# The first stage of a fixed-order decoder layer: squares summed by the matrix product alone, x scaled early, loads on one queue

## The chip, the core and the metric

The kernel runs on one core of one Trainium2 chip, in one launch. TensorE (PE) does the matrix products, ScalarE (ACT) and VectorE (DVE) the elementwise work; DMA transfers are issued by SyncE (SP) and GpSimd (POOL). The metric is the time of one execution on the device in microseconds (us): the median of three runs before the change is 2008.87 us (2008.06 to 2016.31). One execution was profiled: 2006.7 us, of which the span of the trace takes 2004.6 us.

## The reference

One layer of a hybrid decoder on 1024 prompt tokens (one sequence) and 32 sample tokens (8 sequences of 4), width 1024, all in float32. A conditioning vector per sequence gives scale and shift of every norm:

```python
mod = (jax.nn.silu(c) @ w_ada + b_ada).reshape(B, N_MOD, D_MODEL)
hn = modulate(rmsnorm(x, g_ffn1), mod[:, 0], mod[:, 1])       # h * (1 + scale) + shift
x = x + 0.5 * mod[:, 2][:, None, :] * swiglu(hn, w1_gate, w1_up, w1_down)
hn = modulate(rmsnorm(x, g_mix), mod[:, 3], mod[:, 4])
mo, ... = mixer(hn, ...)                                      # recurrence and short convolution
x = x + mod[:, 5][:, None, :] * mo
hn = modulate(rmsnorm(x, g_ffn2), mod[:, 6], mod[:, 7])
x = x + 0.5 * mod[:, 8][:, None, :] * swiglu(hn, w2_gate, w2_up, w2_down)
y = rmsnorm(x, final_gain)
```

`rmsnorm` divides by the root of the mean square over the 1024 channels; `swiglu` is silu(h·Wg)·(h·Wu), times Wd, with 3072 hidden channels.

## The kernel before

Tokens lie along the free dimension (N = 1056, two halves of 528), channels along the 128 partitions in 8 blocks k. Every float32 operand of a large product is split into a high part (ACT copies it, rounded) and a low part (DVE subtracts), and a product is three matrix products: high·high, high·low, low·high. A weight unit of 128x512 is split in the same way (`split_to`, L218 on ACT and L219 on DVE). The hidden channels of the first feed-forward layer are computed in pairs of column blocks. Pairs 1 to 11 go by Strassen's scheme with seven products each (`strassen`, L441): the forms of the activations are, in order, 11, T1, T2, 22, T3, 21, T4 (11, 22 and 21 are quarters of the activations themselves, T1 to T4 are sums of quarters), those of the weights 11, S1, S2, S4, S3, 12, 22, and the seven go into three accumulators a, c, a, c, a, b, a, named `ga_` for the gate and `up_` for the up product. Pair 0 is done directly, in `first_pair()` (L877); the products of its two column blocks are called `first` and `second` in the trace.

`first_pair()` is the first stage, and what the change touches. In the order of the code:

- x is loaded in three pieces (352, 528 and 176 tokens) on POOL's queue (L919); the conditioning weights (`ada`) and the first weights (`wf`) come on SP's queue.
- `norm` (L889): for each block k ACT squares a piece of x (L528), DVE adds the squares into one accumulator (L532, L537), and PE sums it over the partitions with one-column matmuls, three for the first piece, five and two for the others (`nrm`, L551). `stats` then takes mean, root and reciprocal (L554 to L559), puts it on diagonals (`dg`, L565), spreads it over the partitions with a matmul (`rb`, L572), and ACT copies it out (`rall`, L576).
- the conditioning products (`ada`, L485), their transpose and sum into `modT` (L490 to L500).
- for each block k `modulate`: DVE multiplies x by scale and norm in one instruction (L613), ACT adds the shift and rounds to the high part (L615), DVE makes the low part (L616), ACT adds the shift to x itself (L618). The products of this block follow (L906). Blocks 0 and 1 use the first conditioning part, blocks 2 to 4 the second, 5 to 7 the third.
- the silu of the gate (L924, ACT) and the product with up (L926, DVE); T1 and T2 (`token_forms`, L650 to L656) and T3 (`rest_of_forms`); the products of the second column block; its silu and product; T4.

The order in which each engine meets its instructions is set by a scheduler of the framework from dependences and estimated times, not by the order of the code. On each engine instructions then run in that order.

Of the kernel before, what the change touches and what calls it, by code (L numbers as in the profile page):

```python
# [1 line left out]

# [235 lines left out]
def decoder_step(ctx, tc, xin, par, ada0, ada1, ada2, wada, wf, wga, wdn, wdl, wmi, wgt, wmo,  # L238
# [77 lines left out]

    def prompt(span):

        return min(span[0] + span[1], T) - span[0]
# [204 lines left out]
    def square_add(accs, sp, k, new=tmp, fold=False, join=False):  # L524

        xs = x[:, k, of(sp)]
        sq = new(f"sq{sp[0]}_{k}", sp[1])
# [7 lines left out]
        if fold and k == KD - 1:  # L535
            for other in (accs.pop(), accs.pop()):
                dve.tensor_add(accs[0], accs[0], other)  # L537
# [3 lines left out]
    def stats(accs, spans, first, lag, keep=None):  # L541
# [6 lines left out]
        b = bank(f"nrm{name}")  # L548
        for i, (c, s, _) in enumerate(at):
            for n, acc in enumerate(accs[c]):  # L550
                pe.matmul(b[:, i:i + 1], acc[:, s:s + P], ones[:, 0:1], start=n == 0, stop=n == len(accs[c]) - 1)  # L551
# [26 lines left out]
    def modulate_samples(buf, k0, k1, sp, inplace=False):  # L578

        if inplace and (len(x.cuts(k0, k1)) > 1 or k0 < 4 < k1):  # L580
            for a, e in x.cuts(k0, k1):
                for lo, hi in ((a, min(e, 4)), (max(a, 4), e)):
                    if lo < hi:
                        modulate_samples(buf, lo, hi, sp, True)
# [9 lines left out]
        for a, e in x.cuts(k0, k1):  # L594
# [282 lines left out]
    def first_pair():  # L877
        fp = open_pool("firstp", bufs=10)
        firstp.append(fp)
        rall = fp.tile([P, N], F32, name="rall", bufs=1)  # L880
        early, late = FIRST_SPANS[:-1], FIRST_SPANS[-1:]
# [3 lines left out]
        def square(name, width):  # L885
            return fp.tile([P, CH], F32, tag="sq", name=name, bufs=5)[:, :width]

        def norm(spans):
            accs = []  # L889
            for sp in spans:  # L890
                accs.append([])
                for k in range(KD):
                    square_add(accs[-1], sp, k, square, True)
            for _ in stats(accs, spans, 0, 0, keep=rall):
                pass
# [7 lines left out]
        def product(outs, spans, hl, k, j, first, last):  # L903
            for i, (wh, h) in enumerate(((0, 0), (0, 1), (1, 0))):
                for sp in spans:
# [3 lines left out]
        def products(spans, ks, ahead):  # L909
            for k in ks:  # L910
                for w in range(2):
                    product(outs[w], spans, ws.unit(gu[k // 4][w], ahead), k, k % 4, k == 0, k == KD - 1)
# [5 lines left out]
        def load(lo, n):  # L918
            pool.dma_start(x[:, :, lo:lo + n], xin[:, :, lo:lo + n])  # L919

        def swiglu(j, outs):
            m = [(wide if j == 0 else lambda name: tmp(name, HALF))(f"m{j}_{h}") for h in range(2)]
            for sp in FIRST_SPANS:
                act.activation(piece(m, sp), outs[0][sp], AF.Silu)  # L924
            for sp in FIRST_SPANS:
                dve.tensor_mul(piece(m, sp), piece(m, sp), outs[1][sp])  # L926
            return m

        load(0, 352)
        load(352, 528)  # L930
        load(*late[0])
        ada_stream(fp, KD, range(NFIRST), lambda u: (ada0, ada1, ada2)[u[0]][u[1]])
# [11 lines left out]
        lo, n = late[0][0], prompt(late[0])  # L944
        for u in range(NFIRST):
            k1 = k0 + ADA[u][0][4]
            ks = range(k0, k1)
            if u == 0:
                for last, spans in enumerate((early[:1], early[1:])):
                    for k in ks:  # L950
                        for sp in spans:
                            modulate(0, k, sp[0], sp[1], rall[:, of(sp)])
                        if last and k == k1 - 1:
                            norm(late)
                        products(spans, [k], 1)
                        more_ada(2)
                modulate_samples(0, k0, k1, late[0], True)
                for k in ks:
                    modulate(0, k, lo, n, rall[:, lo:T])
                    products(late, [k], 1)  # L960
                ws.raw_bufs = 2
                ws.dma_ahead()
            else:
                modulate_samples(0, k0, k1, late[0], True)
                for k in ks:
                    for a, e in ((0, HALF), (HALF, T)):
                        modulate(0, k, a, e - a, rall[:, a:e])
                    products(FIRST_SPANS, [k], 3 if k >= 4 else 1)
                    if k == k0 and u + 1 < NFIRST:
                        more_ada(KD)  # L970
# [4 lines left out]
        m0 = swiglu(0, outs)  # L975
        forms = {f: form_tile(f, f"hn{f}") for f in ("T1", "T2", "T3")}
        forms.update({"11": hns[0][0][0], "21": hns[0][1][0], "22": hns[0][1][1]})
        for _ in token_forms(forms, 0, HALF):
            pass
        rest_of_forms(forms, ["T3"])  # L980
        outs = [outputs(f"second{w}_") for w in range(2)]
        for w in range(2):
            ids = ws.take("gu1", (1, w))
            for k in range(KD):
# [472 lines left out]
```

## Time and profile before

| | |
|---|---|
| median of three runs | 2008.87 us (2008.06 to 2016.31) |
| profiled execution | 2006.7 us, its span 2004.6 us |
| PE busy | 1942.3 us, 97% of the span |
| DVE, ACT, POOL busy | 1284.5, 768.7, 128.7 us |
| chain of work that ended last | PE 93%, DVE 4%, DMA 2% |
| mean granted clock of PE over the span | 0.991 of full speed |

PE's granted clock is given in tenths or as a share of full speed; its two levels are 1.2 and 2.4 GHz, so 0.50 is the lower and 1.00 the upper. In the page's 40 slices, 50 us each, PE is below nine tenths only in the first two (three and seven tenths) and the last one; DMA moves most in the first slice (278 GB/s). The first stage ends at about 124 us of the span, where the Strassen products of pair 1 begin.

### The profile page before, as it was taken

How to read it: one execution, taken by the hardware profiler on the slowest of the kernel's cores; microseconds unless marked ns; L12 is line 12 of the kernel's file. 1: busy time of each engine (PE TensorE's matmuls, PEld its weight loads, DVE VectorE, ACT ScalarE, POOL GpSimd, SP SyncE). 2: the span in 40 equal slices, each digit the busy share in tenths (PEclk: the TensorE clock that was granted, in tenths of full speed). 3: DMA queues.
4: the chain of work that ended last, by engine and by line, in shares of the span. 5: the costliest groups of instructions: out<-in, count | busy, mean ns of one | idle time of the engine just before them, and what ended most of it. 6: DMA issues, size and time to landing. Idle time of an engine off the chain costs nothing.

```text
span 2004.6 us, 36544 instructions
## 1 busy us (share of the span) xinstructions
PE 1942.3 (97%) x15188; PEld 1912.5 (95%) x15188; DVE 1284.5 (64%) x2549; ACT 768.7 (38%) x1366; POOL 128.7 (6%) x226
## 2 busy tenths in 40 slices
PE   3799999999999999999999999999999999999997
PEld 2699999999999999999999999999999999999997
DVE  4934555565457875584887768666555645878656
ACT  4523223233343422244443447433333333433324
POOL 0000000110010100000000010001000000100000
PEclk8899999999999999999999999999999999999999
DMA  7145545541254523011111122533323223742402
GB/s 278 50 161 172 188 165 177 184 139 65 75 183 163 194 74 130 22 48 53 48 43 53 43 78 76 179 130 106 114 81 102 92 86 107 245 149 92 140 33 87
DMA packets 88773, 230.68 MB, mean 115 GB/s; under 512 B 7792, under 2 KB 40576, under 8 KB 88608
## 3 DMA queue, kind: packets, MB, share of 16 engines
q1 hardware_dynamic: 62512, 133.07, 19.9%
q0 software_dynamic: 26096, 95.28, 13.2%
q8 instruction: 119, 1.95, 0.4%
q14 instruction: 46, 0.38, 0.1%
HBM read 180.63 MB, written 47.69 MB: 114 GB/s over the span
## 4 chain that ended last, share of the span: by engine, by line
PE 93%; DVE 4%; DMA 2%; ACT 1%; issue 0%; SPq 0%; DVEq 0%; ACTq 0%
PE bk L402 14%; PE up_a L441 13%; PE ga_a L441 13%; PE dn_a L441 9%; PE up_c L441 6%; PE ga_c L441 6%; PE dn_c L441 5%; PE ga_b L441 3%; PE up_b L441 3%; PE v L402 2%; PE b L402 2%; PE c L402 2%; PE x L402 2%; PE n L402 2%; PE dn_b L441 2%; PE ada L485 2%
## 5 line engine op out<-in xcount | busy, mean ns | idle before, releaser
L219 DVE TENSOR_TENSOR hl<-raw,hl 128x512 fp32r<-128x512 f32 x286 | 195.0, 686 | 213.5 <-ACT hl L218 213.1
L218 ACT ACTIVATE hl<-raw 128x512 fp32r<-128x512 f32 x286 | 175.9, 625 | 261.3 <-PE bk L402 105.2
L218 ACT ACTIVATE hl<-S_ga 128x512 fp32r<-128x512 f32 x176 | 111.0, 631 | 272.4 <-DVE S_ga L171 55.0
L441 PE MATMUL dn_a<-f,hl 128*128 128x264 f32 x1536 | 191.8, 284 | 0.0
L402 PE MATMUL bk<-ml,hl 128*128 128x352 f32 (+2 forms) x1248 | 189.5, 312 | 2.1 <-DVE x L672 2.1
L441 PEld LDWEIGHTS dn_a<-f,hl 128*128 128x128 f32 x1536 | 189.2, 188 | 0.0
L402 PEld LDWEIGHTS bk<-ml,hl 128*128 128x128 f32 x1248 | 186.5, 188 | 2.6 <-DVE x L672 2.6
L219 DVE TENSOR_TENSOR hl<-S_ga,hl 128x512 fp32r<-128x512 f32 x176 | 121.2, 689 | 84.2 <-ACT hl L218 83.4
L672 DVE SCALAR_TENSOR_TENSOR x<-bk,modT,x 128x352 f32<-128x352 f32 (+6 forms) x160 | 81.3, 533 | 101.1 <-PE bk L402 100.3
L441 PE MATMUL up_a<-hnT,hl 128*128 128x264 f32 x792 | 102.6, 285 | 0.0
L441 PE MATMUL ga_a<-hnT,hl 128*128 128x264 f32 x792 | 102.5, 285 | 0.0
L441 PE MATMUL up_a<-hmT,hl 128*128 128x264 f32 x792 | 102.3, 285 | 0.0
L441 PE MATMUL ga_a<-hmT,hl 128*128 128x264 f32 x792 | 102.3, 285 | 0.0
L441 PEld LDWEIGHTS up_a<-hnT,hl 128*128 128x128 f32 x792 | 98.7, 188 | 2.5 <-ACT u5st L455 0.4
L441 PEld LDWEIGHTS ga_a<-hnT,hl 128*128 128x128 f32 x792 | 98.6, 188 | 2.5 <-ACT g1st L455 0.4
L441 PEld LDWEIGHTS ga_a<-hmT,hl 128*128 128x128 f32 x792 | 98.9, 188 | 0.4 <-ACT g1st L455 0.4
L441 PEld LDWEIGHTS up_a<-hmT,hl 128*128 128x128 f32 x792 | 98.9, 188 | 0.4 <-ACT u1st L455 0.4
L441 PE MATMUL dn_c<-f,hl 128*128 128x264 f32 x768 | 96.4, 284 | 0.0
L441 PEld LDWEIGHTS dn_c<-f,hl 128*128 128x128 f32 x768 | 94.8, 188 | 0.0
L806 DVE TENSOR_TENSOR f<-f 128x1056 fp32r<-128x1056 f32 x56 | 67.9, 1253 | 26.0 <-ACT f L805 26.0
L218 ACT ACTIVATE hl<-S_dn 128x512 fp32r<-128x512 f32 x64 | 40.0, 629 | 112.1 <-PE dn_a L441 30.4
L528 ACT ACTIVATE sq<-x 128x352 f32<-128x352 f32 (+4 forms) x120 | 50.3, 434 | 71.5 <-DVE x L672 52.1
(447 smaller groups left out, 3740.2 us busy)
## 6 DMA issues: line engine op xcount, KB each, us to landing
raw<-wga SPq DMA_DIRECT2D x88, 512.0 KB, 3.4
f<-mf POOLq DMA_DIRECT2D x28, 1056.0 KB, 5.9
raw<-wada SPq DMA_DIRECT2D x56, 512.0 KB, 5.0
raw<-wdn SPq DMA_DIRECT2D x32, 512.0 KB, 3.4
mf<-mt POOLq DMA_DIRECT2D x48, 264.0 KB, 3.3
raw<-wmi SPq DMA_DIRECT2D x20, 512.0 KB, 3.3
ml<-ml POOLq DMA_DIRECT2D x16, 528.0 KB, 5.2
raw<-wdl SPq DMA_DIRECT2D x16, 512.0 KB, 3.3
```

The source lines that it names most:

```text
L218: self.nc.scalar.activation(hl[:, 0], src, AF.Copy)
L219: self.nc.vector.tensor_sub(hl[:, 1], src, hl[:, 0].bitcast(F32))
L402: pe.matmul(b[:, :sp[1]], hl[:, wh, k], rhs(k, h, sp), start=first and k == ks[0] and i == 0, stop=last and k == ks[-1] and i == 2)
L441: pe.matmul(b[:, 512 - Q + q * Q:512 + q * Q], hl[:, wh, k], forms[X_FORMS[i]][:, k, h, q * Q:q * Q + Q], start=new and k == 0 and j == 0, ...
L485: pe.matmul(ada_bank[u][32 * q:32 * q + 32, :ADA_W[u]], cst[:, k], raw[:, q], start=k == 0, stop=k == KD - 1, skip_group_check=True)
L528: act.activation(sq, xs, AF.Square)
L672: dve.scalar_tensor_tensor(x[:, o, lo:lo + n], b[:, :n], modT[:, buf, GATE, o, 0:1], x[:, o, lo:lo + n], op0=ALU.mult, op1=ALU.add)
L806: dve.tensor_sub(form[:, k:k + 2, 1], raw[:, k:k + 2], form[:, k:k + 2, 0].bitcast(F32))
```

## The change

Within `first_pair()` the order of the code becomes the order on ACT, DVE, PE and SP: `in_order` adds a dependence between every two instructions that follow each other on one engine. POOL is left free, and from pair 1 on the scheduler sets the order as before. In this stage x is loaded on SP's queue, in the order x (352 tokens), x (528), a weight unit, x (176), then the conditioning. Each block of squares goes to PE directly: one matmul of one column for every 128 tokens of every block k, accumulated over k, 80 in all, and DVE's additions are gone. As soon as its norm is known x is multiplied by it in place (`scale`), by DVE; `modulate` becomes two ACT instructions with both scale and shift (high part and x itself) and one subtraction on DVE. The four spans of a block k stand together. T1 of the second column block, its silu, T2, T3 and T4 stand in a written order, with the splitting of the next weight units between them. `stats` can be given a bank that is already filled (`b=`), and `modulate_samples` takes `normed=True`, where the multiplication by the norm is left out. The call `more_units(True)` is gone, which gave the first stage two more buffers for split weights.

```diff
@@
+    @contextmanager
+    def in_order(*engines):
+        block = nc.cur_bb
+        last = block.bb.instructions[-1]
+        yield
+        traced = block.bb.instructions
+        first = next(i for i in reversed(range(len(traced))) if traced[i] is last) + 1
+        info = mybir.DependencyInfo(mybir.DependencyClass.NoSync, mybir.DependencyReason.DATA)
+        prev = {}
+        for ins in traced[first:]:
+            if ins.engine in engines:
+                if ins.engine in prev:
+                    tc.add_manual_dep(ins, prev[ins.engine].name, info, reason="in_order")
+                prev[ins.engine] = ins
...
+            def squares(self, k0, k1):
+                for k in range(k0, k1):
+                    sq = fp.tile([P, HALF], F32, tag="sq", name=f"sq{self.lo}_{k}", bufs=4)[:, :self.n]
+                    act.activation(sq, x[:, k, self.lo:self.lo + self.n], AF.Square)
+                    i = 0
+                    for lo, n in self.spans:
+                        for s in range(0, n, P):
+                            at = lo - self.lo + min(s, n - P)
+                            pe.matmul(self.b[:, i:i + 1], sq[:, at:at + P], ones[:, 0:1], start=k == 0 and i == 0,
+                                      stop=k == KD - 1, skip_group_check=True)
+                            i += 1
...
+            def scale(self, k0, k1):
+                xs = x[:, k0:k1, self.lo:self.lo + self.n]
+                r = rall[:, None, self.lo:self.lo + self.n]
+                dve.tensor_mul(xs, xs, r.to_broadcast([P, k1 - k0, self.n]))
...
-        load(0, 352)
-        load(352, 528)
-        load(*late[0])
...
+        def load(norm):
+            nc.sync.dma_start(x[:, :, norm.lo:norm.lo + norm.n], xin[:, :, norm.lo:norm.lo + norm.n])
...
-        norm(early[:1])
-        more_ada(KD)
-        norm(early[1:])
+        na.squares(0, KD)
+        na.roots()
+        na.spread()
+        for u0 in range(NFIRST):
+            na.scale(ADA[u0][0][3], ADA[u0][0][3] + ADA[u0][0][4])
+        nb.squares(0, KD)
+        nd.squares(0, 3)
+        nb.roots()
         ws.split_to(gu[0][1])
+        nd.squares(3, KD)
+        nb.spread()
+        nd.roots()
+        more_ada(KD - 2)
+        nd.spread()
...
+        beside = iter((3, 2, 3, 0, 2, 2, 2, 2, 0, 0) + 6 * (0,))
         for u in range(NFIRST):
...
+            for k in range(k0, k1):
+                for a, e in ((0, HALF), (HALF, T)):
+                    xs, hi = x[:, k, a:e], hn_at(k, 0, a, e - a)
+                    form = dict(scale=modT[:, 0, SCALE, k, 0:1], bias=modT[:, 0, SHIFT, k, 0:1])
+                    act.activation(hi, xs, AF.Identity, **form)
+                    act.activation(xs, xs, AF.Identity, **form)
+                    dve.tensor_sub(hn_at(k, 1, a, e - a), xs, hi.bitcast(F32))
+                    if k == k0 and a == 0:
+                        modulate_samples(0, k0, k1, FIRST_SPANS[3], True, True)
+                if k == k1 - 1 and u + 1 < NFIRST:
+                    for norm in (nb, nd):
+                        norm.scale(k1, k1 + ADA[u + 1][0][4])
...
+                for w in range(2):
+                    product(outs[w], ws.unit(gu[k // 4][w], 0), k, k % 4, k == 0, k == KD - 1)
+                    more_ada(next(beside))
...
+        m0 = silus(0, outs)
+        times(m0, outs)
...
+        for k in range(KD):
+            product(outs[0], ws.unit(ids[0][k // 4], 0), k, k % 4, k == 0, k == KD - 1)
+        ws.split_to(units[-1])
+        for k in range(4):
+            first_sum(k)
+        ws.split_to(units[-1] + 2)
+        m1 = silus(1, outs)
+        for k in range(KD):
+            product(outs[1], ws.unit(ids[1][k // 4], 0), k, k % 4, k == 0, k == KD - 1)
+        for k in range(2):
+            second_sum(k)
+        times(m1, outs)
+        for k in range(2, 4):
+            second_sum(k)
+        ws.split_to(units[-1] + 3)
+        for k in range(2):
+            third_sum(k)
+        ws.split_to(units[-1] + 4)
+        for k in range(2, 4):
+            third_sum(k)
+        ws.split_to(units[-1] + 5)
         forms["T4"] = form_tile("T4", "hnT4")
         rest_of_forms(forms, ["T4"])
-        more_units(False)
...
-    more_units(True)
-    forms, (m0, m1) = first_pair()
+    with in_order(engine.Activation, engine.DVE, engine.PE, engine.SP):
+        forms, (m0, m1) = first_pair()
```

`first_sum` makes and splits T1, `second_sum` T2 and the sum that T4 is split from, `third_sum` T3.

What this moves can be seen in the order of the instructions. On PE, the program's start, before the change (`sq` are the accumulated squares, of which one is left for each piece of x; `nrm` the sums, `rb` the spread norm):

```order
L551 MATMUL nrm_163<-ones,sq_0_140 128x1 x3
L572 MATMUL rb_178<-dg_174,ones 128x128 x2
L572 MATMUL rb_178<-dg_174,ones 128x96
L485 MATMUL ada_183<-raw_118,cst 32x128 x4
...
L551 MATMUL nrm_284<-ones,sq_0_238 128x1 x2
L551 MATMUL nrm_284<-ones,sq_0_261 128x1 x3
L572 MATMUL rb_304<-dg_297,ones 128x128
L572 MATMUL rb_304<-dg_297,ones 128x48
```

and after it:

```order
L916 MATMUL nrm_112<-ones,sq_0_142 128x1 x3
L916 MATMUL nrm_112<-ones,sq_1_147 128x1 x3
...
L916 MATMUL nrm_112<-ones,sq_7_177 128x1 x3
L588 MATMUL rb_193<-dg_189,ones 128x128 x2
L588 MATMUL rb_193<-dg_189,ones 128x96
L916 MATMUL nrm_113<-ones,sq_0_201 128x1 x5
...
L916 MATMUL nrm_113<-ones,sq_7_250 128x1 x5
L916 MATMUL nrm_114<-ones,sq_0_257 128x1 x2
...
L916 MATMUL nrm_114<-ones,sq_7_307 128x1 x2
L588 MATMUL rb_311<-dg_276,ones 128x128
```

The ten one-column matmuls became eighty, one set for every square, and the conditioning products stand behind all of them.

On PE, the gate products of pair 1 before the change (`hn_111` is form 11, `hnT_793` T1, `hnT_794` T2, `hn_112` 22, `hnT_795` T3, `hn_113` 21, `hnT_1075` T4; the other operand is the split weight):

```order
L441 MATMUL ga_a<-hn_111,hl_855 128x264 x24
L441 MATMUL ga_c<-hnT_793,hl_908 128x264 x24
L485 MATMUL ada_1188<-raw_1092,cst 32x256 x4
L485 MATMUL ada_1188<-raw_1094,cst 32x256 x4
L441 MATMUL ga_a<-hnT_794,hl_961 128x264 x24
L441 MATMUL ga_c<-hn_112,hl_1014 128x264 x24
L441 MATMUL ga_a<-hnT_795,hl_1150 128x264 x24
...
L441 MATMUL ga_b<-hn_113,hl_1201 128x264 x24
L441 MATMUL ga_a<-hnT_1075,hl_1230 128x264 x24
```

and after it (`hn_108` is 11, `hnT_776` T1, `hnT_777` T2, `hn_109` 22, `hnT_778` T3, `hn_110` 21, `hnT_1078` T4):

```order
L459 MATMUL ga_a<-hn_108,hl_915 128x264 x24
L459 MATMUL ga_c<-hnT_776,hl_920 128x264 x24
L459 MATMUL ga_b<-hn_110,hl_1190 128x264 x17
...
L459 MATMUL ga_a<-hnT_777,hl_1051 128x264 x8
...
L459 MATMUL ga_a<-hnT_777,hl_1051 128x264 x16
L459 MATMUL ga_c<-hn_109,hl_1062 128x264 x24
L459 MATMUL ga_a<-hnT_778,hl_1073 128x264 x24
...
L459 MATMUL ga_b<-hn_110,hl_1190 128x264 x7
L459 MATMUL ga_a<-hnT_1078,hl_1219 128x264 x24
```

The product of form 21, with weight `hl_1190`, stood sixth and now stands third, ahead of those of T2, 22 and T3.

On DVE, after the change, from the product of the second block's silu and up (L958) to the split of that weight (`x_70` on both sides is a sum written back; `S_ga` are sums of weights, `hl` their low parts, `hnT` low parts of the forms):

```order
L958 TENSOR_TENSOR m_1_924<-m_1_924,second_2_794 128x176
L1035 TENSOR_TENSOR t2f_1039<-x_70,t1f_907 128x528
L683 TENSOR_TENSOR hnT_777<-t2f_1039,hnT_777 128x528
L1037 TENSOR_TENSOR x_70<-x_70,t2f_1039 128x528
...
L1037 TENSOR_TENSOR x_70<-x_70,t2f_1044 128x528
L174 TENSOR_TENSOR S_ga_4_0_1049<-S_ga_4_0_918,raw_707 128x512
L220 TENSOR_TENSOR hl_1051<-S_ga_4_0_1049,hl_1051 128x512
L1040 TENSOR_TENSOR x_70<-x_70 128x528
L683 TENSOR_TENSOR hnT_778<-x_70,hnT_778 128x528
...
L220 TENSOR_TENSOR hl_1073<-S_ga_4_0_1071,hl_1073 128x512
L683 TENSOR_TENSOR hnT_1078<-x_70,hnT_1078 128x528 x4
L220 TENSOR_TENSOR hl_1190<-raw_897,hl_1190 128x512
```

Between these stand further T2, T3 and weight sums, 26 rows with 29 instructions in all from the first product L958 to `hl_1190`; before the change the sums of T1, T2 and T3 stood ahead of the first block's product L926 (a row `L667 TENSOR_TENSOR hnT_795<-x_70,hnT_795 128x528 x3` was the last of them).

## Rows read from the trace of the kernel before

**Rows 1.** The page, busy time of each engine, share of the span, instructions

```profile
PE 1942.3 (97%) x15188; PEld 1912.5 (95%) x15188; DVE 1284.5 (64%) x2549; ACT 768.7 (38%) x1366; POOL 128.7 (6%) x226
```

**Rows 2.** Waits of PE, 0 to 130 us: engine, line, waited for, us, times, longest

```profile
PE nrm L551 <- DVE sq L537: 21.3, 3, 16.2
PE second L906 <- ACT m L924: 9.4, 1, 9.4
```

**Rows 3.** Timeline of PE, 8 to 126 us: start, us, engine, line, op, tiles, shape, count [idle before]

```profile
16.22 1.41 PE L551 MATMUL nrm<-ones,sq 128*128 128x1 f32 x6 [16.22 <-DVE sq L537]
27.44 1.59 PE L572 MATMUL rb<-dg,ones 128*128 128x128 f32 x6 [9.81 <-DVE dg L565]
28.97 3.64 PE L485 MATMUL ada<-raw,cst 128*32 128x128 f32 x64
33.27 0.60 PE L551 MATMUL nrm<-ones,sq 128*128 128x1 f32 x4 [0.66 <-DVE sq L537]
...
44.48 2.11 PE L906 MATMUL first<-hn,hl 128*128 128x352 f32 x6
...
55.47 0.86 PE L485 MATMUL ada<-raw,cst 128*32 128x192 f32 x16
...
69.80 16.59 PE L906 MATMUL first<-hn,hl 128*128 128x352 f32 x120
...
96.03 28.42 PE L906 MATMUL second<-hn,hl 128*128 128x352 f32 x190 [9.36 <-ACT m L924]
```

**Rows 4.** Stretches of PE: from:to, us, busy (instructions), granted clock, DMA share, GB/s

```profile
0.00:16.20 16.20, 0.00 (x0) 1.00 0.90 318
...
60.20:67.00 6.80, 6.54 (x24) 0.50 0.00 0
...
96.00:101.20 5.20, 5.17 (x21) 0.50 0.14 54
```

**Rows 5.** Timeline of PE, 120 to 180 us

```profile
124.29 3.14 PE L441 MATMUL ga_a<-hn,hl 128*128 128x264 f32 x24
127.27 3.08 PE L441 MATMUL ga_c<-hnT,hl 128*128 128x264 f32 x24
...
131.28 3.19 PE L441 MATMUL ga_a<-hnT,hl 128*128 128x264 f32 x24
```

**Rows 6.** Timeline of ACT, 0 to 30 us

```profile
11.32 3.23 ACT L528 ACTIVATE sq<-x 128x352 f32<-128x352 f32 x8 [5.87 <-DMA x<-xin]
```

**Rows 7.** Timeline of all engines, 49 to 62 us

```profile
52.49 0.16 DVE L554 TENSOR_SCALAR sm<-nrm 128x2 f32<-128x2 f32 x1 [1.70 <-PE nrm L551]
...
54.80 0.32 ACT L576 ACTIVATE rall<-rb 128x176 f32<-128x176 f32 x1 [1.91 <-PE rb L572]
...
56.84 0.37 DVE L490 STREAM_TRANSPOSE adat<-ada 128x192 f32<-128x192 f32 x1
...
58.42 0.18 DVE L500 TENSOR_TENSOR modT<-modT,pv 128x27 f32<-128x27 f32 x1
```

**Rows 8.** Instruction groups by shape on ACT: busy us, mean ns

```profile
L615 ACT ACTIVATE hn<-x,modT 128x528 fp32r<-128x528 f32 x6 | 4.4, 736 | 3.5 <-DVE x L613 3.5
...
L666 ACT ACTIVATE hnT<-t2f 128x528 fp32r<-128x528 f32 x4 | 2.5, 636 | 1.1 <-DVE t2f L652 1.1
```

**Rows 9.** The same on ACT, whole span (two per-partition operands, then one)

```profile
L1068 ACT ACTIVATE xc<-xl,pv 128x352 f32<-128x352 f32 x8 | 5.3, 683 | 1.2 <-DVE q L1159 0.8 <-DVE h L1155 0.4
...
L1068 ACT ACTIVATE cs<-ul,pv 128x352 f32<-128x352 f32 x8 | 4.4, 585 | 4.8 <-DVE ul L1195 4.8
```

**Rows 10.** Instruction groups by shape on DVE, 0 to 130 us

```profile
L652 DVE TENSOR_TENSOR t2f<-x,t1f 128x528 f32<-128x528 f32 x4 | 2.8, 701 | 0.8 <-ACT x L618 0.8
...
L926 DVE TENSOR_TENSOR m<-m,second 128x352 f32<-128x352 f32 x2 | 1.0, 517 | 2.2 <-PE second L906 2.2
```

**Rows 11.** Timeline of DVE, 79 to 97 us

```profile
81.01 0.70 DVE L667 TENSOR_TENSOR hnT<-t1f,hnT 128x528 fp32r<-128x528 f32 x1
81.62 0.70 DVE L652 TENSOR_TENSOR t2f<-x,t1f 128x528 f32<-128x528 f32 x1
```

More of the change, by code (lines that the diff above doesn't have):

```diff
@@ L1 @@
 from collections import deque
+from contextlib import contextmanager
 import numpy as np
@@ L534, in square_add, with stats @@
             dve.tensor_add(accs[0], accs[0], accs.pop())
[L535 to L537 removed]
     rs = {}
[L541 removed]
+    def stats(accs, spans, first, lag, keep=None, b=None):
         at = [(c, min(P * i, sp[1] - P), P * i) for c, sp in enumerate(spans) for i in range((sp[1] + P - 1) // P)]
@@ L547, in stats @@
             yield
[L548 to L551, printed above, removed]
+        if b is None:
+            b = bank(f"nrm{name}")
+            for i, (c, s, _) in enumerate(at):
+                for n, acc in enumerate(accs[c]):
+                    pe.matmul(b[:, i:i + 1], acc[:, s:s + P], ones[:, 0:1], start=n == 0, stop=n == len(accs[c]) - 1)
         sm = tp.tile([P, 3, 9], F32, tag="sm", name=f"sm{name}", bufs=2)
@@ L880, in first_pair, with __init__, roots, spread @@
         rall = fp.tile([P, N], F32, name="rall", bufs=1)
-        early, late = FIRST_SPANS[:-1], FIRST_SPANS[-1:]
         h11, h22, h21 = (form_tile(f, f"hn{f}") for f in ("11", "22", "21"))
         hns[0] = [[h11, form_tile("T4", "hn12")], [h21, h22]]
[L885 to L895, printed above, removed]
+        class Norm:
+            def __init__(self, spans):
+                self.spans, self.lo, self.n = spans, spans[0][0], sum(n for _, n in spans)
+                self.b = bank(f"nrm{self.lo}")
+            def squares(self, k0, k1):
[9 more added lines that the diff above has]
+                            i += 1
+            def roots(self):
+                self.steps = stats(None, self.spans, 0, 1, keep=rall, b=self.b)
+                next(self.steps)
+            def spread(self):
+                for _ in self.steps:
+                    pass
+            def scale(self, k0, k1):
+                xs = x[:, k0:k1, self.lo:self.lo + self.n]
+                r = rall[:, None, self.lo:self.lo + self.n]
+                dve.tensor_mul(xs, xs, r.to_broadcast([P, k1 - k0, self.n]))
         def outputs(name):
@@ L901, in outputs, with product @@
                     FIRST_SPANS[3]: b[2][:, 256:432]}
-        def product(outs, spans, hl, k, j, first, last):
+        def product(outs, hl, k, j, first, last):
             for i, (wh, h) in enumerate(((0, 0), (0, 1), (1, 0))):
-                for sp in spans:
+                for sp in FIRST_SPANS:
                     pe.matmul(outs[sp], hl[:, wh, j], hn_at(k, h, *sp), start=first and i == 0 and sp != FIRST_SPANS[3],
                               stop=last and i == 2, skip_group_check=True)
[L909 to L912, printed above, removed]
         def piece(t, sp):
@@ L942, in first_pair @@
+        nd.roots()
+        more_ada(KD - 2)
+        nd.spread()
+        nb.scale(0, ADA[0][0][4])
+        nd.scale(0, ADA[0][0][4])
+        more_ada(2)
         outs = [outputs(f"first{w}_") for w in range(2)]
+        beside = iter((3, 2, 3, 0, 2, 2, 2, 2, 0, 0) + 6 * (0,))
         k0 = 0
-        lo, n = late[0][0], prompt(late[0])
         for u in range(NFIRST):
             k1 = k0 + ADA[u][0][4]
[L947 to L970, printed above, removed]
```

58 lines of the change are left out of this document (39 added, 19 removed).

## The prediction

> **What bounds the kernel now.** I read the page's busy times first: PE is busy 97% of the span [rows 1], so a gain can only come from a stretch where it waits, and what delays it elsewhere is paid in full, since nothing later has slack to take it back. Then the waits of PE in the first 130 us: 21.3 us for the accumulated squares and 9.4 us in one piece for a silu on ACT [rows 2]. The timeline of PE shows where they lie [rows 3]. The norms end with the first product at 44.48 us. The 120 matmuls from 69.80 on close the first pair at 86.4 us, then come the idle 9.36 us, and the second pair starts at 96.03. Pair 1 starts at 124.29, and its third product at 131.28 [rows 5]. That third product is the place by which I measure, because from there on the order of the kernel before and after is nearly the same.
>
> PE's clock has to be read beside it. After the 9.36 us without work the second pair ran at 0.50 until 101.2 us, and the same is seen from 60.2 to 67.0 us [rows 4]. 0.50 is the level of 1.2 GHz, 1.00 that of 2.4. A stretch of 6.8 us at the lower level does the work of 3.4.
>
> **The way to the first product.** Removed are DVE's additions of squares, the three separate loads on POOL's queue and the wait of PE for accumulated squares. Added are 70 one-column matmuls. Such a sum costs 0.47 us when PE comes out of idleness (three in 1.41 us at 16.22) and 0.30 us later (two in 0.60 us at 33.27, after the 3.64 us of conditioning products that stand in front of it) [rows 3]. These are my bounds; no row shows a long stream of them.
>
> - The first piece of x, 1.44 MB, now has only 0.28 MB of parameters ahead. At the 318 GB/s of the first 16 us [rows 4] both take 5.4 us; with issue and first bytes I take 8 us. The upper bound is the 11.32 us of now [rows 6]. Issuing on SP instead of POOL has no other effect that I charge: nothing computes on SP, and the conditioning loads queued behind x are only needed after the norms.
> - The first square takes 0.40 us (3.23/8 [rows 6]). PE then does 24 sums at 0.47, as it comes from idleness: 11.3 us, until 19.7. ACT needs 3.2 us for the same eight squares, so PE is the slower one.
> - The root, diagonals and spread took from 52.49 to 55.12 us [rows 7], 2.6 us, and about 0.7 more with the spread at the lower clock (0.53 a matmul at 27.44 [rows 3] against the 0.30 of a sum): 23.0. ACT has a fixed order now, and behind the waiting copy of the norm stand the squares of the second piece. Before, other squares were done in such a wait. So the 40 sums of the second piece begin at 23.6. I take 0.30 each, since PE then has no idle stretch: 12.0 us, until 35.6. The 16 of the third add 4.8: 40.4.
> - Five spread matmuls 1.5, eight conditioning steps at 0.43 (two in 0.86 at 55.47 [rows 3]) 3.4, the last spread 0.6, transpose to modT 1.8 (56.84 to 58.60 [rows 7]), the first high part 0.8: the first product at about 48, against 44.48. What DVE saved lay beside PE's 11.3 + 12.0 + 4.8 us and buys nothing.
>
> A page bears on the choice of 0.30: the Trainium skill, "TensorE: Matmul & The Clock Gate", section "What's actually happening", says that the throttled level is the default and that sustained activity releases it. Rows 3 show the same for the conditioning products before 33.27; whether one-column sums count as activity no row shows. By the page's rule the sum stands or is up to 4 us lower; if they don't count, the second rival holds.
>
> **The first pair.** It has 192 matmuls at 0.138 us (16.59/120 [rows 3]): 26.4 us, and beside them 16 conditioning steps of 0.43: 6.9. ACT's part of a block k is four instructions. With a shift alone they take 0.736 for 528 columns [rows 8]; a second operand for each partition adds 0.10 (683 against 585 ns [rows 9]), so some 0.82, spaced by about 0.1 less: 2.9 us, just under PE's 3.3 for the block. In the steady part ACT is therefore hidden. At the first block of each of the three conditioning parts it isn't: the written order has high part, x, then the samples' high part, which waits for DVE's low part and two sample operations, and only then the other half's two. The second matrix product of the block needs the last low part. That is 0.8 + 0.8 + 0.7 + 0.4 + 0.3 + 0.8 + 0.8 + 0.7 = 5.3 us, for which PE holds 1 us of work: 4.3 us idle, three times, 13 us. For the second and third part the block before gives no cover, since the first instruction there waits for modT, which waits for conditioning products that stand beside that block on PE. I add 3.4 us of lower clock after one of the three waits; bounds are none and all three. Sum 26.4 + 6.9 + 13 + 3.4 = 49.7, against 41.9 before. The pair ends at 97.7.
>
> **The second pair.** Silu and its table load now come directly behind ACT's last block instead of behind the sums, so the 9.36 us wait goes. What is late next is nothing on PE: 26.4 us, end at 124.1, as before (124.29).
>
> **Pair 1.** T2, T3 and T4 stand on DVE behind the product of silu and up, which waits for the second pair's end. Before, T1 to T3 were done at 81 to 95 us, one DVE instruction every 0.62 us [rows 11], and this was what delayed the silu. Now they stand between PE and its third product, whose weight `hl_1190` is split last of all. The order between them has sum, copy on ACT, low part, again and again, each waiting for the other engine. From the end of the second pair: four products 1.7 (0.52 for 352 columns [rows 10]); two second sums of 0.70 + 0.64 + 0.62 + 0.62 = 2.6 [rows 8, 10]; one weight sum with its split 1.9; four third sums of 0.70 + 0.64 + 0.62 = 1.96, in all 7.8; two weight sums 3.8; four T4 low parts 2.5, their copies ahead on ACT; the split 0.6. Sum 23.5 us. PE has two products ready, 7.0 us (124.29 to 131.28 [rows 5]), and then idles for 16.5. Bounds: 18 us if every one of the 29 DVE instructions follows at 0.62, 26 if each hand-over adds 0.1. The third product starts at 124.1 + 23.5 = 147.6 instead of 131.28: 16.3 us later. It starts at the lower clock, as after the 9.36 us now: 3.4 us more. Once it has begun, T2, T3, T4 and their weights are all ready, so no second wait follows. The two split buffers that are gone cost nothing of their own: six units are split by then and six buffers are there; without that cover the seventh waits for the first product, which is long done.
>
> Sum: 16.3 + 3.4 = 19.7 us on the profiled 2006.7 gives 2026.4. The median of the runs lies 2.2 us above that execution: 2028.6.
>
> **Rivals.** (1) All 80 sums run at 0.47: 56 x 0.17 = 9.5 us more, 2038. For it speaks that PE's three sums at 16.22 ran at that pace; against it that they are three. (2) The block order bites less than I reckon: the sample operations are small, and if two of three waits vanish with their lower clock, the pair lasts 42 us, as now. Then the third product is at 139, and the sum is 11 us: 2020; with the wait of pair 1 at its lower bound of 18 us, 2014, within 0.5% (I count 10 us as the least that a measurement tells from no change). (3) Faster: the early norm lets the first pair run as one stream. First product 44 with all sums at 0.30, pair 33.3, second pair 26.4: end at 103.7. With 18 us behind it the third product is at 121.7, 9.6 us earlier than now, and at 2.4 GHz without the later stretch: 1999. It decides if the second pair ends before 103 us. Against it: ACT and DVE hand every block over in turn, and any one of the three waits spoils it. (4) No change at all, as the lost 9.36 us wait and the new one cancel: needs pair 1's third product at 131, that is the second pair ended by 108; 2009.
>
> **Chances.** Forecast 0.55 (2018 to 2036), rival 1 0.17, rivals 2 and 4 0.17 together, of which most is within 0.5%, rival 3 0.11. Faster by over 0.5% (below 1998.8): 0.11; within: 0.18; slower: 0.71. The range reaches from 2004, between rivals 3 and 4 and the unknown costs, to 2041, above rival 1.
>
> **What would show it.** In the profile after: nrm rows of three at 1.4 us first, then five at 1.5; the first product near 48 us; three idle stretches of 4 us in front of the first, third and sixth block, named by ACT; no wait at the start of the second pair; the third product of pair 1, `ga_b`, with an idle time of some 16 us in front that ends with DVE's split. If that last wait is under 5 us, the forecast is wrong by its main term. If the five sums take 2.35 us, rival 1 holds.

## The result, and the profile after

The changed kernel takes 2042.74 us (2040.30 to 2042.93, four runs), the kernel before on the same chip 2012.25 (2008.06 to 2016.31): a ratio of 1.0149, 95% interval 1.0121 to 1.0177, slower by 30.5 us. The kernel before spreads over 10 us from run to run, and its profiled execution, 2006.7, is a low one; the profiled execution after took 2042.9, so between the two traces there are 36.3 us of span (2004.6 to 2040.9).

The page's first row after, to be read against [rows 1]: the engines, busy time, share of the span.

```profile
PE 1983.0 (97%) x15328; PEld 1949.5 (96%) x15328; DVE 1274.1 (62%) x2502; ACT 771.1 (38%) x1350; POOL 126.0 (6%) x223
```

PE is busy 41 us more. The 70 added sums are 30 us of it at 0.43 each; the rest is the same matmuls as before taking longer, as they do at the lower clock. Waits of PE in the first 170 us (engine, line, waited for, us in total, times, longest), against [rows 2]:

```profile
PE ga_b L459 <- ACT hl L219: 15.5, 1, 15.5
PE nrm L916 <- ACT sq L911: 11.7, 2, 10.7
PE first L943 <- ACT hn L1004: 9.4, 5, 3.3
PE first L943 <- DVE hn L1006: 2.4, 4, 1.2
...
```

The 9.4 us wait for the silu is gone, and a wait of 15.5 us stands in pair 1, as forecast. PE's waits have not grown in all, though: counting the small ones left out above, they add up to 41.9 us, and to 45.8 before (13.1 of them for the diagonals `dg`, which [rows 2] doesn't show). The time went into PE's busy stretches, as its timeline shows (start, us, line, tiles, count), against [rows 3, 5]:

```profile
10.65 10.37 PE L916 MATMUL nrm<-ones,sq 128*128 128x1 f32 x48 [10.65 <-ACT sq L911]
...
25.32 24.05 PE L916 MATMUL nrm<-ones,sq 128*128 128x1 f32 x112 [1.08 <-ACT sq L911]
...
57.14 0.51 PE L943 MATMUL first<-hn,hl 128*128 128x352 f32 x2 [2.20 <-ACT hn L1004]
60.12 1.31 PE L943 MATMUL first<-hn,hl 128*128 128x352 f32 x4 [2.47 <-ACT hn L1004]
...
77.56 1.31 PE L943 MATMUL first<-hn,hl 128*128 128x352 f32 x4 [3.32 <-ACT hn L1004]
...
111.09 26.25 PE L943 MATMUL second<-hn,hl 128*128 128x352 f32 x192
138.37 3.17 PE L459 MATMUL ga_a<-hn,hl 128*128 128x264 f32 x24 [1.03 <-DVE m L958]
...
160.02 0.81 PE L459 MATMUL ga_b<-hn,hl 128*128 128x264 f32 x2 [15.55 <-ACT hl L219]
```

The 24 sums of the first piece take 10.37 us, 0.43 each, and the 56 of the others 24.05, again 0.43 each, not 0.30. The first product comes at 57.14 us, against 44.48 before. The first pair lasts 53.95 us, the second 26.25, and the third product of pair 1 starts at 160.02 instead of 131.28, 28.7 us later. The first up product is 32.9 us later (180.39 against 147.49). Of the 4.2 us between, some 2.7 are the lower clock at which PE started after its wait (an estimate: 5.34 us of work at a clock of 0.50 from 159.9 to 165.7 us), 1.1 are two conditioning steps that stood ahead of the third product before, and 0.3 is a second short wait. The last 3.4 us come much later, and I return to them at the end.

### The profile page after: what moved, and what is told of

Its sections match the earlier page's. It is cut to its first block, busy times and chain, and to the rows that moved or that the text cites. A ratio compares the mean times of both kernels' runs of the same rounds, so it can differ in the third digit from the quotient of the medians.

```text
span 2040.9 us, 36758 instructions
## 1 busy us (share of the span) xinstructions
PE 1983.0 (97%) x15328; PEld 1949.5 (96%) x15328; DVE 1274.1 (62%) x2502; ACT 771.1 (38%) x1350; POOL 126.0 (6%) x223
## 4 chain that ended last, share of the span: by engine, by line
PE 95%; DVE 3%; ACT 1%; DMA 0%; issue 0%; DVEq 0%; SPq 0%; ACTq 0%
PE bk L420 13%; PE up_a L459 13%; PE ga_a L459 13%; PE dn_a L459 9%; PE up_c L459 6%; PE ga_c L459 6%; PE dn_c L459 5%; PE ga_b L459 3%; PE up_b L459 3%; PE dn_b L459 2%; PE v L420 2%; PE b L420 2%; PE c L420 2%; PE x L420 2%; PE n L420 2%; PE ada L503 2%
## 5 line engine op out<-in xcount | busy, mean ns | idle before, releaser
L821 ACT ACTIVATE f<-f 128x1056 fp32r<-128x1056 f32 x56 | 57.7, 1078 | 45.5 <-DMA f<-mf 44.8
```

Of the source, the lines that this page charges most:

```text
L821: act.activation(form[:, k:k + 2, 0], raw[:, k:k + 2], AF.Copy)
```

## Experiments

All times are medians of several runs, where nothing else is said; the kernel before took 2012 to 2013 us beside each group. The edits are to the changed kernel.

**DVE adds the squares (e1).**

```diff
                     act.activation(sq, x[:, k, self.lo:self.lo + self.n], AF.Square)
+                    if k < 2:
+                        self.accs.append(sq)
+                        continue
+                    dve.tensor_add(self.accs[k % 2], self.accs[k % 2], sq)
+                    if k < KD - 1:
+                        continue
                     i = 0
...
-                            pe.matmul(self.b[:, i:i + 1], sq[:, at:at + P], ones[:, 0:1], start=k == 0 and i == 0,
-                                      stop=k == KD - 1, skip_group_check=True)
+                            for j, acc in enumerate(self.accs):
+                                pe.matmul(self.b[:, i:i + 1], acc[:, at:at + P], ones[:, 0:1], start=j == 0,
+                                          stop=j == 1)
```

> DVE adds the squares of the eight blocks into two accumulators again, so PE does 20 one-column sums instead of 80; all else is as after the change. Theory A (the sums at 0.43 us each are what the first stage lost): the first sums end near 17 us instead of 21, those of the second and third piece near 33 instead of 49; with root, spread and conditioning the first product comes at 42 to 46 us instead of 57, and the run takes 2027 to 2032 us, 11 to 15 less than the changed kernel. Rival B (something else holds the first product, the loads of the conditioning or the fixed order on ACT): the first product stays after 52 us, and the run takes 2037 or more.

Measured: 2030.44 us (2029.86 to 2031.04), 12.3 less than the changed kernel. PE's timeline there:

```profile
13.60 2.69 PE L924 MATMUL nrm<-ones,sq 128*128 128x1 f32 x12 [13.60 <-DVE sq L916]
...
26.77 4.63 PE L924 MATMUL nrm<-ones,sq 128*128 128x1 f32 x20 [7.27 <-DVE sq L916]
36.43 1.95 PE L924 MATMUL nrm<-ones,sq 128*128 128x1 f32 x8 [5.03 <-DVE sq L916]
...
46.15 0.51 PE L951 MATMUL first<-hn,hl 128*128 128x352 f32 x2 [2.20 <-ACT hn L1012]
```

PE now waits for DVE between the sums, and is still done at 38.4 instead of 49.4. The first product comes 11 us earlier. A sum still costs 0.45 us here (six in 2.69), but there are 20 of them. Theory A holds for the run and, within 0.2 us, for the first product; the later sums, expected to end near 33 us, ended at 38.4, because of the waits for DVE.

**Filling PE's idle time ahead of the sums (e4).** 14 matmuls of 128 columns before `na.squares`:

```diff
+        wb = bank("warm")
+        for i in range(14):
+            pe.matmul(wb[:, :P], ones, ones, start=True, stop=True)
         na.squares(0, KD)
```

> The changed kernel with 14 matmuls of 128 columns (ones by ones, into a bank nothing reads) ahead of the first sums, in PE's idle time before 10.65 us: about 0.53 us each, 7.4 us. Theory A (the one-column sums don't hold the upper clock, whatever came before): after these matmuls the first sums may take 0.30 us, but within some us they are at 0.43 again, those of the second and third piece from the start; the first product comes at 54 to 57 us. Rival B (the sums ran slowly only because PE came from idleness): 24 sums take 7 us instead of 10.4, the other 56 take 17 instead of 24, and the first product comes at 46 to 49 us.

Measured: 2041.43 us in one run, the first product at 57.36. Timeline of PE, and the granted clock in stretches (from:to, us, busy, clock, DMA share, GB/s):

```profile
0.99 5.91 PE L980 MATMUL warm<-ones 128*128 128x128 f32 x28 [0.99 <-POOL ones L358]
10.15 10.40 PE L916 MATMUL nrm<-ones,sq 128*128 128x1 f32 x48 [3.25 <-ACT sq L911]
...
24.85 24.05 PE L916 MATMUL nrm<-ones,sq 128*128 128x1 f32 x112 [1.08 <-ACT sq L911]
```

```profile
4.00:7.00 3.00, 2.90 (x16) 1.00 1.03 321
7.00:10.10 3.10, 0.00 (x0) 0.94 1.02 331
10.10:13.00 2.90, 2.85 (x14) 0.50 1.05 395
...
30.00:40.00 10.00, 10.00 (x48) 0.50 0.00 0
40.00:48.90 8.90, 8.90 (x43) 0.50 0.18 60
```

24 us without a gap on PE, all of it one-column sums, ran at 0.50 to the end. Rival B falls. The added matmuls did reach the upper clock, though only at their end. Each matmul is two instructions; until 5.6 us each of them takes 421 ns or more, and the last ones, in the view of durations (ns: least, median, most), down to 275:

```profile
L980 PE MATMUL warm<-ones x7: 275/291/421, 5.6 to 6.6; 128*128 128x128 f32 x7
```

PE was then idle for 3.25 us, and the clock fell in that gap (0.94 on the mean from 7.0 to 10.1 us), so that the first sums again started at 0.50. This run therefore doesn't show whether sums would *keep* an upper clock; sums later in the program bear on that, and stand at the end of the next section.

**No fixed order (e2).**

```diff
-    with in_order(engine.Activation, engine.DVE, engine.PE, engine.SP):
+    with in_order():
```

> The changed kernel without the fixed order: the same instructions, the scheduler sets the order. Theory A (the written order costs the first pair its waits and pair 1 its long wait, the sums the rest): the sums stay at 0.43 and the first product near 57 us; the first pair lasts 42 to 46 us instead of 54, as before the change; there is no single wait of 15 us in pair 1, its seven gate products end after 28 to 32 us instead of 42; the run takes 2018 to 2026 us. Rival B (the work between ACT and DVE is the cost, in whatever order): the pair lasts over 50 us and the gate of pair 1 over 38; the run takes 2038 or more.

Measured: 2017.08 us (2013.75 to 2019.99), 1.0024 times the kernel before (1.0010 to 1.0037): 25.7 us of the 30.5 come back with the same instructions in another order, just beyond theory A's 2018. PE's timeline:

```profile
56.17 1.35 PE L943 MATMUL first<-hn,hl 128*128 128x352 f32 x3 [3.39 <-ACT hn L1004]
...
96.57 26.25 PE L943 MATMUL second<-hn,hl 128*128 128x352 f32 x192
122.65 3.13 PE L459 MATMUL ga_a<-hn,hl 128*128 128x264 f32 x24
130.10 4.67 PE L459 MATMUL ga_c<-hnT,hl 128*128 128x264 f32 x24 [4.32 <-DVE m L958]
```

The sums and the first product (56.17) are as after the change. The first pair takes 40.4 us instead of 53.95, and instead of 15.5 us in pair 1 there is one wait of 4.3 (and one of 0.8 for a load).

**ACT and DVE free, PE and SP fixed (e10)** (`in_order(engine.PE, engine.SP)`).

> The changed kernel with the order fixed on PE and SP alone; ACT and DVE are the scheduler's. Theory A (the fixed order of ACT and DVE costs, since each waits with other ready work behind it): the run comes to within 10 us of e2's 2017, 2017 to 2027; pair 1's gate takes under 30 us instead of 42. Rival B (the fixed order on PE and SP costs as much): 2032 or more.

Measured: 2024.00 us (2022.72 to 2030.88); theory A holds. The gate of pair 1 takes 25.3 us, up to the first up product, without a wait inside; a shorter wait stands ahead of it:

```profile
135.47 5.47 PE L459 MATMUL ga_a<-hn,hl 128*128 128x264 f32 x24 [6.88 <-DVE m L958]
160.76 3.10 PE L459 MATMUL up_a<-hn,hl 128*128 128x264 f32 x24
```

Of the 25.7 us, 18.7 come back with ACT and DVE free, and the other 7 when PE and SP are free as well. The opposite order, PE and SP free first, was not tried.

**The order inside a block (e9).** Both high parts first, then the samples, then x and the low parts:

```diff
+                for xs, hi, _ in parts:
+                    act.activation(hi, xs, AF.Identity, **form)
+                if k == k0:
+                    modulate_samples(0, k0, k1, FIRST_SPANS[3], True, True)
+                for xs, hi, low in parts:
+                    act.activation(xs, xs, AF.Identity, **form)
+                    dve.tensor_sub(low, xs, hi.bitcast(F32))
```

> The changed kernel, fixed order kept, with the block's steps written in another order: both high parts first, then the samples, then x for both halves and the low parts. Theory A (ACT waiting for the samples' DVE steps between the two halves makes the first pair long): the idle before each conditioning part falls by about 2 us, three times, and some of the lower clock behind it goes: the first pair lasts 45 to 50 us instead of 54, the run takes 2033 to 2039 us. Rival B (what makes the pair long is modT's late arrival or ACT's amount of work): the pair stays over 52 us, the run over 2040.

Measured: 2035.46 us (2033.05 to 2038.13), 7.3 less. The second pair starts at 106.44 us, the first product at 58.19, so the first pair took 48.2 us, as theory A had it. The hand-over that it removes looks like this in the changed kernel (ACT and DVE; in brackets the idle time ahead and who ended it), at the third block:

```profile
72.85 0.83 ACT L1004 ACTIVATE hn<-x,modT 128x528 fp32r<-128x528 f32 x1 [8.86 <-DVE modT L518]
73.72 0.83 ACT L1005 ACTIVATE x<-x,modT 128x528 f32<-128x528 f32 x1
...
74.58 0.71 DVE L1006 TENSOR_TENSOR hn<-x,hn 128x528 fp32r<-128x528 f32 x1 [1.76 <-ACT x L1005]
...
75.71 0.26 ACT L619 ACTIVATE hn<-x 128x64 fp32r<-128x64 f32 x1 [1.17 <-DVE x L613]
...
76.72 0.79 ACT L1004 ACTIVATE hn<-x,modT 128x496 fp32r<-128x496 f32 x1
```

From 74.55 to 76.72 ACT does nothing but two small copies, each behind a step of DVE, while the second half's high part, which needs neither, stands behind them.

**The place of the product with `hl_1190` (e3 and e5).** In the changed kernel it stood third, the weight's split last. Fixing PE's order for this gate puts it sixth:

```diff
-            strassen([(f"ga{p}", ws.take(f"ga{n}", (p, 0))[0], gate)], forms, 4)
+            with in_order(*([mybir.EngineType.PE] if (n, p) == (1, 1) else [])):
+                strassen([(f"ga{p}", ws.take(f"ga{n}", (p, 0))[0], gate)], forms, 4)
```

> The changed kernel, with the order on PE fixed for the gate products of pair 1 too: 11, T1, T2, 22, T3, 21, T4, so that the product with weight hl_1190 stands sixth instead of third. Theory A (DVE's chain of sums behind the second pair bounds this place, not the order on PE): the wait of 15.5 us breaks into three or four of 2 to 4, the first up product still starts at 178 to 184 us, and the run takes 2040 to 2046 us. Rival B (the place of that product is the cost): the up products start 10 us or more earlier and the run takes 2033 or less.

Measured: 2048.00 us (2045.22 to 2051.09), slower than the changed kernel by 5, the up products at 183.14. But PE's wait there was for something else: 20.0 us for a conditioning load (`raw<-wada`), which SP issued only at 158 us. So the run doesn't tell the two theories apart. In e5 the conditioning steps come behind T3's product (`i in (4, 5)` for this gate instead of `i % 3 == 1`):

> As e3_pe_order, with the conditioning steps of this gate moved behind its T3 product, so that PE doesn't meet a load that is issued late. Theory A (DVE's chain bounds the place): T2's product starts near 146 us, when its weight is split, T3's at 156 to 158, between them waits of 2 to 4 us, and the first up product starts at 173 to 178 us instead of 180; the run takes 2035 to 2041 us. Rival B (the order on PE is the cost): the up products start before 170 us and the run takes 2030 or less.

Measured: 2050.86 us (2046.47 to 2053.05). Both theories miss. PE's longest wait, and what ACT did at its end:

```profile
163.16 5.15 PE L459 MATMUL ga_a<-hnT,hl 128*128 128x264 f32 x24 [17.07 <-ACT g1st L473]
```

```profile
160.97 1.65 ACT L219 ACTIVATE hl<-raw 128x512 fp32r<-128x512 f32 x3
162.53 0.58 ACT L473 ACTIVATE g1st<-ga_a 128x528 f32<-128x528 f32 x1
```

T2's sums and weight were ready near 147 us (145.8 in the changed kernel, where the stage runs 1.6 us earlier), yet its product waited until 163 for `g1st` (L473): the first accumulator has to be copied out before T2's product is added into it, and this copy stands on ACT behind the whole chain of T2, T3, T4 and the weight splits. The scheduler's odd third product goes to another accumulator, b, and so needs no copy. Its place was not the cause but a way around: in the changed kernel too ACT copies the first accumulator only at 160.91 us, so T2's product could not have started before 161.5, against 160.02 for the one that stood there.

**The sums of T2 and T3 beside the second pair (e6).**

```diff
         for k in range(4):
             first_sum(k)
+        for k in range(4):
+            second_sum(k)
+        for k in range(4):
+            third_sum(k)
...
-        for k in range(2):
-            second_sum(k)
         times(m1, outs)
-        for k in range(2, 4):
-            second_sum(k)
...
-        for k in range(2):
-            third_sum(k)
...
-        for k in range(2, 4):
-            third_sum(k)
```

> The changed kernel with the sums of T2 and T3 written right behind those of T1, beside the second pair's gate product, ahead of its silu; S2, S4, S3 and T4 stay where they are. Theory A (the chain of sums between ACT and DVE behind the second pair's end is what PE waits for): the 15.5 us wait is gone or under 4 us; the silu of the second pair is later by some us, so pair 1 starts 4 to 6 us later than 138.4; its up products start at 168 to 173 us instead of 180; the run takes 2030 to 2036 us. Rival B (the work is only moved, and what it delays costs the same): up products at 178 or later, run 2040 or more.

Measured: 2034.60 us (2031.38 to 2040.39), 8.1 less. The 15.5 us wait is gone, and the first up product starts at 169.55 us, so theory A holds. What the early sums delay, the second pair's silu and its product with up, costs part of the gain back:

```profile
142.18 4.83 PE L459 MATMUL ga_a<-hn,hl 128*128 128x264 f32 x24 [7.14 <-DVE m L958]
...
150.39 0.51 PE L459 MATMUL ga_b<-hn,hl 128*128 128x264 f32 x2 [0.46 <-ACT hl L219]
```

**The queue of the loads (e8)** (`pool.dma_start` for the three pieces of x).

> The changed kernel with the three loads of x issued on POOL's queue, as before the change. Theory A (which queue issues them matters little; being ahead of the conditioning matters some): x shares the DMA engines with the conditioning again, the first sums start at 11 to 13 us instead of 8.7 to 10.7, and the first product comes 1 to 4 us later. Rival B (the queue is worth more): the first product comes over 5 us later or earlier.

Measured: 2042.10 us in one run. The first sums start at 12.34 us, in the kernels with SP loads and the same sums at 8.62 to 10.84, and the first product at 59.70, 2.6 later than in the changed kernel. That fits theory A; in the time of the one run nothing of it can be seen.

**The parts together.** Free order, DVE's additions, early sums (e7):

> Three edits together: no fixed order, DVE's accumulation of squares (two accumulators, 20 sums), sums of T2 and T3 written early. Theory A (the parts are separate and add up): 12.3 us of e1 and 25.7 of e2 from 2042.7, and some 4 us for the rest of the wait in pair 1: 1998 to 2006 us; first product at 44 to 46 us, second pair's end near 112, first up product at 137 to 142 us against 147.5 before; faster than the kernel before by 5 to 14 us. Rival B (the free order gains by hiding what the sums cost, so the two overlap): 2010 or more, the first pair again over 46 us long.

Measured: 2002.54 us (1995.99 to 2005.73), ratio to the kernel before 0.9952 (0.9935 to 0.9970), faster by 10 us, at the expected place.

```profile
88.90 26.05 PE L951 MATMUL second<-hn,hl 128*128 128x352 f32 x190 [1.21 <-ACT m L961]
...
137.72 3.10 PE L459 MATMUL up_a<-hn,hl 128*128 128x264 f32 x24
```

Without the early sums (e11):

> Free order and DVE's accumulation of squares, without the early sums of T2 and T3: e7 less one edit. Theory A (the two parts add up and the early sums are worth a few us on top): 2042.7 - 12.3 - 25.7 = 2004.7, so 2002 to 2008, 1 to 5 us above e7. Rival B (the early sums are what makes e7 faster than the kernel before): 2010 or more.

Measured: 2005.92 us (2005.67 to 2011.11), 0.9971 (0.9958 to 0.9985). And with the block order added to e7 (e12):

> e7 with e9's order of a block's steps written as well (the scheduler is free to change it). Theory A (without the fixed order the scheduler already puts both high parts ahead of x, so the written order there is worth nothing more): 2000 to 2006 us, within 4 us of e7's 2002.5. Rival B (the written order still counts, as the scheduler takes it into account): the first pair falls under 38 us and the run under 1998.

Measured: 2003.03 us (2000.24 to 2004.33), 0.9948 (0.9928 to 0.9968), the same as e7. The free order needed no hint. What e11 keeps of the change is the early scale, x on SP's queue, `modulate` with two operands on ACT, two accumulators of squares instead of one, the written order of the code as far as the scheduler heeds it, and two split buffers fewer. Together they are worth 6 us against the kernel before, and were not tried one by one. With them the parts add up: 12.3 and 25.7 us of loss less these 6 make about 32, and 30.5 were measured.

## Why the prediction was wrong, step by step

The direction was right, and so were the new wait in pair 1 and the lost wait for the silu; the size was not: 2028.6 forecast, 2042.7 measured, 1.7 us above the range's end. Two terms of the sum failed, each by about 7 us: the price of the sums, and the lower clock in the first pair. By this sum, with either one right the time would have been inside the range. In the terms of the sum:

| term | forecast | measured |
|---|---|---|
| first sums begin | 8.4 us | 10.65 |
| 24 sums of the first piece | 11.3 | 10.37 |
| 56 sums of the others | 16.8 | 24.05 |
| first product at | 48 | 57.14 |
| first pair | 49.7 | 53.95 |
| of it PE's waits | 13 | 9.6 |
| of it lost to the lower clock | 3.4 | some 10 |
| second pair | 26.4 | 26.25 |
| its end to the third product | 23.5 | 22.7 |
| lower clock behind the wait | 3.4 | 4.2 (2.7 of it clock) |
| later | 0 | 3.4 |

The misses add up to the 16.5 us between the forecast for a profiled execution, 2026.4, and the one measured, 2042.9; the medians lie 14.1 apart.

- The first failing step is "I take 0.30 each, since PE then has no idle stretch". The one row with 0.30 stood behind conditioning products, [rows 3] at 33.27, and I carried its rate over to a stream of sums. PE had no idle stretch, as forecast, but the clock stayed at its lower level all the same: the sums ran at 0.43 throughout, 7.3 us more. That was rival 1, at 2038 by its own working, and the other misses came on top of it. (Where the prediction says of the page that "the second rival holds", the first is meant.) The price at the upper level could have been read from a longer row. Later in the trace of the kernel before, nine such sums between products (two instructions each) take 2.06 us, 0.23 each, at a granted clock of 1.00; the 0.43 of the stream at 0.50 is nearly twice that.

```profile
855.62 2.06 PE L551 MATMUL nrm<-ones,sq 128*128 128x1 f32 x18
```

  The page cited there, the Trainium skill's "TensorE: Matmul & The Clock Gate", section "What's actually happening", says that sustained activity releases the clock; by it I leaned to the lower price. The trace disagrees for this kind of work: 24.05 us without a gap at the slow rate, and the granted clock at 0.50 beside it in e4. The measurement decides.
- The load of x landed 2.3 us later than I took (within its bounds), which the runs vary by as well: 8.62 to 10.84.
- The second failing step is "I add 3.4 us of lower clock after one of the three waits". Of the 11.8 us of waits for `hn` above, 2.2 lie ahead of the first product, so the pair's own waits are 9.6 us, less than the 13 forecast. But the clock was low behind all three:

```profile
57.10:111.00 53.90, 44.18 (x319) 0.81 0.29 101
```

0.81 on the mean over 53.9 us is some 20 us at the lower level. The stretches in which it lies, with PE's busy time as the second number:

```profile
59.80:66.70 6.90, 6.36 (x39) 0.51 0.58 208
76.90:83.80 6.90, 6.01 (x32) 0.51 0.22 76
94.00:97.40 3.40, 3.40 (x16) 0.50 0.00 0
100.80:104.30 3.50, 3.50 (x17) 0.51 0.00 0
```

That is 19.3 us of work, which at the upper level would take half, so some 10 us are lost (an estimate). The busy time says nearly the same: 44.2 us against the 33.3 of the forecast's matmuls at the upper level, 10.9 more. I had named "all three", 10 us, as the upper bound. In e2 the same stage has the lower clock only from 56.1 to about 62.
- ACT's price per instruction came out as estimated from [rows 8, 9]: 0.82 us with two operands for each partition.

```profile
L1004 ACT ACTIVATE hn<-x,modT 128x528 fp32r<-128x528 f32 x8 | 6.5, 818 | 19.8 <-DVE modT L518 10.4 <-DVE x L932 9.4
```

- The wait in pair 1: 15.55 us against 16.5. The chain runs at the pace I took from the rows, one hand-over after the other (DVE and ACT, the idle time in brackets):

```profile
138.39 0.70 DVE L1035 TENSOR_TENSOR t2f<-x,t1f 128x528 f32<-128x528 f32 x1
139.12 0.65 ACT L682 ACTIVATE hnT<-t2f 128x528 fp32r<-128x528 f32 x1 [10.69 <-DVE t2f L1035]
139.80 0.71 DVE L683 TENSOR_TENSOR hnT<-t2f,hnT 128x528 fp32r<-128x528 f32 x1 [0.71 <-ACT hnT L682]
```

The size was right; what I had wrong is why PE has to wait there. I took the split of `hl_1190` for the cause, and the products behind it as ready. They were ready by then; but e5 shows that another order on PE would have met the copy of the first accumulator, which the same chain holds up on ACT. The place is bound by the order on ACT and DVE, with either product next on PE; with that order free (e10) or the sums early (e6) the 15.5 us are gone, and waits of 6.9 and 7.1 us ahead of pair 1 take their place.
- "Nothing later has slack": the 32.9 us at the first up product are still 33.4 at 640 us and 33.3 at 1228. The other 3.1 arise between 1200 and 1300 us, where PE's clock falls twice in the profiled run after, each time for some 3.5 us in which PE is busy; the lower clock costs about half of that:

```profile
1228.09 2.07 PE L567 MATMUL nrm<-ones,sq 128*128 128x1 f32 x18
```

```profile
1228.00:1230.10 2.10, 2.10 (x22) 1.00 0.31 111
1230.60:1234.10 3.50, 3.50 (x19) 0.51 0.00 0
1268.10:1271.70 3.60, 3.60 (x19) 0.53 0.44 146
```

The second fall comes behind a wait of 1.6 us for `dg`. The first comes behind nine one-column sums, with PE busy without a gap. A fall within 1.5 us of nine such sums, without a gap, stands in the traces of e1, e2, e3, e9 and e12 too. So a busy PE didn't always keep the upper clock over such sums. In e7 and in the kernel before, PE has the same sums and the same wait, and the clock stays up (e7, with the wait at 1220.7 us):

```profile
1200.00:1250.00 50.00, 48.17 (x395) 1.00 0.21 70
```

What decides whether it falls is not shown. I take it for one of the things that spread the runs of one kernel over 10 us; that wasn't tested.

## What to carry to other kernels

A fixed order on engines that hand work to each other puts every wait in front of all that stands behind it; before writing one, go through each engine's list and ask at each wait which later row was ready. Price a small matmul at the clock at which it will run: its rate behind other work, at the upper level, isn't that of a stream which starts at the lower one. And where a wait looks like one instruction's place, ask what the next candidate would have waited for.

## What the runs showed of the hardware

One-column sums, each with its own load of 128x128 weights, cost 0.43 us each on PE in a stream of 24 us at a granted clock of 0.50 (e4), 0.45 to 0.49 in the short groups behind an idle time, 0.30 in groups of two that stood behind products or conditioning steps, and 0.23 in groups of nine between products at a clock of 1.00. They didn't bring the upper clock in 24 us without a gap; 14 matmuls of 128 columns, from idleness too, did (e4).

In the changed kernel the granted clock reads 1.00 over the sums (25.3 to 49.3 us) although they ran at 0.43; in e4 it reads 0.50 over the same sums at the same pace. I read it so that the recorded value says nothing until the first change is recorded. Two other places fit this reading: in the kernel before the sums at 16.22 took 0.47 us under a reading of 1.00, and in e4 the added matmuls went from 421 ns to 275 with no change in it. By this reading the durations tell the clock ahead of the first change, and its row doesn't.
